# A two-layer mixer and MLP network: modulation sections 3 and 4 computed during attention, branch products spaced by gates, the context's last two MLP groups summed in PSUM

## The chip, the cores and the metric

The kernel runs on one core of a Trainium2 chip. The metric is the device time of one execution in microseconds (us), the median of several runs. The engines are named as in the profile: PE (TensorE, matrix products), DVE (VectorE), ACT (ScalarE), POOL (GpSimd) and SP (SyncE, which issues the DMAs, in order, from one queue).

## What is computed

512 latent tokens and 256 context tokens, 1024 wide, pass through two layers. Each layer has a mixing part with three branches (pooling, windowed attention whose latent queries also read the context, and a convolution module), merged by sigmoid gates, and a dense MLP. Both are modulated by six vectors that a product of the conditioning vector with `w_mod` gives.

```python
for i in range(DEPTH):                              # 2 layers
    mod_l = silu_c @ w_mod[i] + b_mod[i]            # six sections of 1024; mod_c likewise
    hl = _modulate(xl, sh1_l, sc1_l)                # layer norm, scale, shift
    ul_pool, ul_q, ul_k, ul_v, ul_conv, ul_gate = _split_in(hl @ w_in[i] + b_in[i])
    ...
    # _merge: (g_pool * y_pool + g_attn * y_attn + g_conv * y_conv) @ w_out
    xl = _post_norm(xl, g1_l, yl, ln1_g[i], ln1_b[i])
    yl = _mlp(_modulate(xl, sh2_l, sc2_l), w_mlp1[i], b_mlp1[i], w_mlp2[i], b_mlp2[i])
    xl = _post_norm(xl, g2_l, yl, ln2_g[i], ln2_b[i])
    # the context stream does the same in layer 0 only
```

## The kernel before

**Products.** Activations lie transposed in two parts, high and low (`actah`, `actal` and `actbh`, `actbl`), each weight tile likewise (`wh` by ACT, L134; `wl` by DVE or POOL, L137, as `ring["on"]` says). Each product is three matmuls: high by high, low by high, high by low. L156 is the matmul of `mm_a_steps`, whose output has features on the partitions: 512 latent tokens in one 512-column matmul, the context in a 256-column one. L165 to L167 are `mm_b_steps`, with tokens on the partitions. Raw weights come in tiles of 256 KB (`raw`, L129).

**Order on PE.** The order is made while the program is written out. Work comes as generators that yield the matmul columns they have issued; `tick` counts them. `later(cols, steps)` puts a generator in a list to be resumed once that many columns have passed. `pace(steps, every)` takes one step of a side generator every so many columns. `cover(cols)` issues steps of `other` (the gates and branch products) for so many columns.

**Modulation.** `mod_steps` (L173) multiplies one section of `w_mod` with the conditioning vector: eight chunks of k, and in each four matmuls of 32 by 256 (L185) into four strips of one PSUM bank; `chunk()` gives the tile for the weights. In layer 0, section 2 is paced through the first part of the mixing, and sections 3 and 4 through the tail stage (L824), in tiles of 512 KB; the six chunks left at its end follow in one run of 24 matmuls (L838).

**Mixing.** `w_phase` runs projections, rotary embedding and splits of q (L676, L677) and k (L710 to L714) on DVE and ACT, starts the convolution (53 scalar-tensor operations a stream on DVE, L323), and issues `other` until that is through. `pool_products` (L722) has its own small products. Then attention blocks run two at a time, their steps interleaved with `other`. The iterator `gated_steps` (L624) first makes eight gates for the attention branch and stores them (`sgd`), then alternates a gate of 24 matmuls a stream (`gate_steps`; bank of `psg`, evicted by ACT's tanh, L611) with a branch product of the pooling or the convolution branch (`branch_steps`; bank of `psa`, evicted by DVE, L621, the gate applied at once). In layer 1 two pooling gates are made ahead (`ahead`). POOL adds the two gated products (L641), and SP stores the sum (`mfd`, L642). Behind attention comes what I call the tail stage: `other` is drained, and eight attention branch products are made (L827 to L835).

**MLP.** `m_phase` runs `mlp1` (features on partitions, relu squared by ACT and DVE) and `mlp2` (tokens on partitions, summed group by group into `acc`, L970) for eight groups of four feature tiles (`GRP`). At the last group but one the sum is multiplied with the gate (L972, DVE) and the residual added (L973, POOL); at the last group follow L976, L977, statistics (L981) and `post`, the layer norm, and `norm_mod`, the modulation for the next layer, whose chain goes DVE (`rs`, L261), POOL (L262), DVE (L263), ACT (L278), PE transposes (L285). In layer 0 the latent tiles are finished first (`outer=True`), and the context's tiles 4 and 5 get groups 7 and 6 behind them (L1038, L1041).

## Time and profile before

| | us |
|---|---|
| runs, median (lowest, highest; 3 runs) | 1978.15 (1974.14, 1978.68) |
| profiled execution, its own time | 1975.67 |
| its span in the trace | 1973.9 |
| PE busy in it | 1848.6 (94%) |
| DVE, POOL, ACT busy | 1200.3, 771.6, 730.8 |
| stage: mixing of layer 0 up to the convolution's end, attention, tail stage | about 0 to 205, 205 to 478, 478 to 544 |
| stage: mixing of layer 1 | about 1212 to 1530 |

PE is busy for 94 percent of the span, and the chain that ended last runs through PE most of the time. A group of instructions is read as line, engine, operation, output from inputs, shape, count. In a wait the receiving instruction stands on the left of the arrow and what released it on the right. In a window, busy time stands engine by engine with its count, then the granted clock as a share of 2.4 GHz (0.50 is 1.2 GHz).

### The profile page before, as it was taken

How to read it: one execution, taken by the hardware profiler on the slowest of the kernel's cores; microseconds unless marked ns; L12 is line 12 of the kernel's file. 1: busy time of each engine (PE TensorE's matmuls, PEld its weight loads, DVE VectorE, ACT ScalarE, POOL GpSimd, SP SyncE). 2: the span in 40 equal slices, each digit the busy share in tenths (PEclk: the TensorE clock that was granted, in tenths of full speed). 3: DMA queues.
4: the chain of work that ended last, by engine and by line, in shares of the span. 5: the costliest groups of instructions: out<-in, count | busy, mean ns of one | idle time of the engine just before them, and what ended most of it. 6: DMA issues, size and time to landing. Idle time of an engine off the chain costs nothing. (4 is left out here: it accounts for less than half of the span.)

```text
span 1973.9 us, 27007 instructions
## 1 busy us (share of the span) xinstructions
PE 1848.6 (94%) x9910; PEld 1548.4 (78%) x9910; DVE 1200.3 (61%) x2067; ACT 730.8 (37%) x1359; POOL 771.6 (39%) x629
## 2 busy tenths in 40 slices
PE   6999899899899999999999988999988989999997
PEld 4788788787678888888788868777866768888886
DVE  6489655654478946865533584786575784333356
ACT  4432255353234422233133344434444354333331
POOL 3653432322434422222122546664342554333343
PEclk8999999999999999999999989999999989999999
DMA  8523111114865434464422423141212753332341
GB/s 304 176 90 118 62 59 46 53 44 154 281 219 190 161 112 133 155 213 143 146 62 86 129 96 105 61 149 63 69 65 96 260 189 118 96 96 86 107 129 43
DMA packets 117557, 244.94 MB, mean 124 GB/s; under 512 B 14608, under 2 KB 16944, under 8 KB 117424
## 3 DMA queue, kind: packets, MB, share of 16 engines
q1 hardware_dynamic: 117424, 243.21, 38.0%
q8 instruction: 78, 1.28, 0.3%
q14 instruction: 55, 0.45, 0.1%
HBM read 223.20 MB, written 19.96 MB: 123 GB/s over the span
## 5 line engine op out<-in xcount | busy, mean ns | idle before, releaser
L137 POOL TENSOR_TENSOR wl<-raw,wh 128x512 fp32r<-128x512 f32 x371 | 516.7, 1405 | 783.6 <-ACT wh L134 698.9
L134 ACT CAST wh<-raw 128x512 fp32r<-128x512 f32 x506 | 310.8, 621 | 596.0 <-PE ps L167 292.1
L156 PE MATMUL ps<-actbh,wh 128*128 128x512 f32 (+1 forms) x1016 | 353.4, 348 | 14.3 <-DVE sg L621 6.9
L156 PE MATMUL ps<-actbl,wh 128*128 128x512 f32 (+1 forms) x1016 | 348.3, 343 | 3.1 <-POOL actbl L251 3.1
L156 PE MATMUL ps<-actbh,wl 128*128 128x512 f32 (+1 forms) x1016 | 347.8, 342 | 2.7 <-DVE rs L261 1.3
L156 PE MATMUL ps<-actah,wh 128*128 128x512 f32 (+1 forms) x928 | 331.4, 357 | 13.7 <-ACT actah L248 4.7
L156 PE MATMUL ps<-actal,wh 128*128 128x512 f32 (+1 forms) x928 | 327.4, 353 | 3.3 <-DVE actal L1097 1.9
L156 PE MATMUL ps<-actah,wl 128*128 128x512 f32 (+1 forms) x928 | 326.9, 352 | 0.4 <-POOL wl L137 0.3
L156 PEld LDWEIGHTS ps<-actbh,wh 128*128 128x128 f32 x1016 | 194.5, 191 | 45.2 <-DVE sg L621 10.0
L156 PEld LDWEIGHTS ps<-actbh,wl 128*128 128x128 f32 x1016 | 194.4, 191 | 25.6 <-DVE wl L137 2.4
L156 PEld LDWEIGHTS ps<-actbl,wh 128*128 128x128 f32 x1016 | 194.6, 192 | 23.3 <-POOL actbl L251 3.8
L156 PEld LDWEIGHTS ps<-actah,wh 128*128 128x128 f32 x928 | 177.5, 191 | 43.8 <-ACT actah L248 5.1
L156 PEld LDWEIGHTS ps<-actal,wh 128*128 128x128 f32 x928 | 177.6, 191 | 25.6 <-DVE actal L1097 2.2
L156 PEld LDWEIGHTS ps<-actah,wl 128*128 128x128 f32 x928 | 177.4, 191 | 24.2 <-POOL wl L137 1.0
L165 PE MATMUL ps<-wh,actah 128*128 128x512 f32 x480 | 192.6, 401 | 2.2 <-DVE acc L977 2.0
L167 PE MATMUL ps<-wh,actal 128*128 128x512 f32 x480 | 190.5, 397 | 3.5 <-DVE actal L251 3.5
L166 PE MATMUL ps<-wl,actah 128*128 128x512 f32 x480 | 190.1, 396 | 0.0
L137 DVE TENSOR_TENSOR wl<-raw,wh 128x512 fp32r<-128x512 f32 x135 | 127.8, 947 | 99.9 <-ACT wh L134 97.3
L204 DVE SCALAR_TENSOR_TENSOR wm<-wm,sc,wm 128x512 f32<-128x512 f32 x140 | 124.4, 924 | 67.1 <-DMA wm<-in_wmod 67.0
L970 DVE TENSOR_TENSOR acc<-ps,acc 128x512 f32<-128x512 f32 x140 | 94.7, 684 | 95.3 <-PE ps L167 95.2
L165 PE MATMUL ps<-wh,actbh 128*128 128x512 f32 (+1 forms) x328 | 127.2, 388 | 1.5 <-DVE fg L621 1.5
L166 PE MATMUL ps<-wl,actbh 128*128 128x512 f32 (+1 forms) x328 | 126.8, 387 | 1.0 <-POOL wl L137 1.0
(207 smaller groups left out, 2721.7 us busy)
## 6 DMA issues: line engine op xcount, KB each, us to landing
raw<-in_w SPq DMA_DIRECT2D x264, 256.0 KB
raw<-in_win SPq DMA_DIRECT2D x154, 256.0 KB
wm<-in_wmod SPq DMA_DIRECT2D x72, 512.0 KB
raw<-in_wout SPq DMA_DIRECT2D x56, 256.0 KB
wm<-in_wmod SPq DMA_DIRECT2D x48, 256.0 KB
raw<-in_wbr SPq DMA_DIRECT2D x32, 256.0 KB
x1d<-R SPq DMA_DIRECT2D x10, 512.0 KB
acc<-in_b SPq DMA_DIRECT2D x10, 512.0 KB
```

What stands on the lines that cost most here:

```text
L134: S.copy(wh, r)
L137: e.tensor_tensor(out=wl, in0=r, in1=wh[:].bitcast(F32), op=ALU.subtract)
L156: T.matmul(ps, w(hl, w0 + n), x[xi][:, k, sl], start=(start and first and hl == 0 and xi == 0), stop=(stop and last and hl == 1))
L165: T.matmul(ps, x[0][:, k0 + k, tsl], wh, start=(k == 0), stop=False)
L166: T.matmul(ps, x[0][:, k0 + k, tsl], wl, start=False, stop=False)
L167: T.matmul(ps, x[1][:, k0 + k, tsl], wh, start=False, stop=(k == n - 1))
L204: V.scalar_tensor_tensor(out=o, in0=x, scalar=sc[:, k, r:r + 1], in1=o, op0=ALU.mult, op1=ALU.add)
L970: V.tensor_add(a, ps, a)
```

## The change

Six edits belong together.

- Sections 3 and 4 of layer 0 leave the tail stage. They are paced at 3500 columns through the attention of layer 0, in weight tiles of 256 columns (128 KB, three buffers), and `mod_steps` yields behind every matmul when tiles are that small, so each of the 64 stands by itself.
- A branch product is cut into pieces (one stream each), put in the list `pend`, and issued one piece behind each gate portion, into a bank of `psg`. The two gates that layer 1 made ahead are gone.
- The high copies of q and k move from DVE to ACT, and the low part of k is subtracted once and copied by ACT the second time.
- `context_end` runs groups 7 and 6 of tiles 4 and 5 into four PSUM banks without a sum in between; `finish` is what stood at the end of `mlp2`.
- In layer 1 a fifth tile of `w1` is computed on each half of the tokens at the beginning of the MLP (`NEXTRA` 8 instead of 6).
- The attention's `t1` shares a buffer, and `ot` has one instead of two.

```diff
@@ -43,7 +43,7 @@
 W_PT = 5000
 W_CN = 10000
 W_PV = 1800
-NEXTRA = (4, 6)
+NEXTRA = (4, 8)
 W_CHAIN = ((51000, 33000, 45000, 45000, 45000, 45000),
            (30000, 42000, 30000, 30000),
@@ -66,6 +66,7 @@
 ON_C = "G"
 MODVC = ()
 W_VAL = 9000
+EV_MOD = 3500
 W_CONV0 = 145000
 W_CONV1 = 118000
 T_POOL, T_Q, T_K, T_V, T_A, T_B, T_G = 0, 2, 6, 7, 8, 10, 12
@@ -158,13 +159,13 @@
                              stop=(stop and last and hl == 1))
                 yield 3 * (sl.stop - sl.start)
-    def mm_b_steps(ps, x, k0, n, tsl, w, cs=slice(0, 512)):
+    def mm_b_steps(ps, x, k0, n, tsl, w, cs=slice(0, 512), start=True, stop=True):
         for k in range(n):
             wh, wl = w[k][0][:, cs], w[k][1][:, cs]
-            T.matmul(ps, x[0][:, k0 + k, tsl], wh, start=(k == 0), stop=False)
+            T.matmul(ps, x[0][:, k0 + k, tsl], wh, start=(start and k == 0), stop=False)
             T.matmul(ps, x[0][:, k0 + k, tsl], wl, start=False, stop=False)
-            T.matmul(ps, x[1][:, k0 + k, tsl], wh, start=False, stop=(k == n - 1))
+            T.matmul(ps, x[1][:, k0 + k, tsl], wh, start=False, stop=(stop and k == n - 1))
             yield 3 * (cs.stop - cs.start)
     modT = {}
@@ -184,6 +185,8 @@
                 o = (j * q) % w.shape[-1]
                 T.matmul(ps[32 * j:32 * j + 32, :q], sc[:, k, :], w[:, o:o + q],
                          start=(k == 0), stop=(k == KD - 1))
+                if w.shape[-1] == q and j < 3:
+                    yield
             yield
         mod_finish(i, s, c0, n, ps, row)
         yield
...
@@ -591,7 +595,7 @@
             psg = ph.enter_context(tc.tile_pool(name=f"psg{i}", bufs=2, space=PSUM, reuse_waits="tile"))
             pss = mix.enter_context(tc.tile_pool(name=f"pss{i}", bufs=2, space=PSUM, reuse_waits="tile"))
             if todo:
-                pace((x for s in todo for x in mod_steps(i, s, 0, D, lambda: mg.tile(
+                pace((x for s in todo[:1] for x in mod_steps(i, s, 0, D, lambda: mg.tile(
                     [P, W], F32, tag="sg", name=uid("wm"))[:, :512])), 10000, 20000)
             def proj(t, sls):
@@ -600,7 +604,10 @@
                 drain(mm_a_steps(w, A, range(KD), o))
                 return [x[0] for x in o]
-            def gate_steps(m, b):
+            pend = []
+
+            def gate_steps(m, b, w2=None, ks=(), done=None):
+
                 t = KD * b + m
                 w = weight_a(I["win"][i, T_G + t])
@@ -609,12 +616,22 @@
                     ps = bank(psg)[:, :sl.stop - sl.start]
                     yield from mm_a_steps(w, A, range(KD), [(ps, sl)])
                     S.activation(g[:, sl], ps, AF.Tanh, bias=bg[:, t:t + 1], scale=0.5)
+                    if pend:
+                        yield from pend.pop(0)
+                if w2:
+                    pend.extend(piece(w2, ks, ks[0], g, o, done if o is outs_all[-1] else None)
+                                for o in outs_all)
                 return g
-            def branch_steps(w, ks, w0, g, outs, pool):
-
+            def piece(w, ks, w0, g, o, done):
                 while ks[0] not in mixed:
                     yield None
+                yield from branch_steps(w, ks, w0, g, [o], psg)
+                if done:
+                    done(g)
+
+            def branch_steps(w, ks, w0, g, outs, pool):
+
                 for _, sl in outs:
                     ps = bank(pool)[:, :sl.stop - sl.start]
                     yield from mm_a_steps(w, B, ks, [(ps, sl)], w0)
@@ -626,22 +643,26 @@
                     g = yield from gate_steps(m, 1)
                     nc.sync.dma_start(out=sgd[m], in_=g)
-                w, d, e, ahead = {}, {}, {}, 0 if todo else 2
-                for m in range(ahead):
-                    d[m] = yield from gate_steps(m, 0)
+                w, d = {}, {}
+
+                def merge(m, e):
+                    G.tensor_tensor(out=d[m], in0=d[m], in1=e, op=ALU.add)
+                    nc.sync.dma_start(out=mfd[m], in_=d.pop(m))
+
                 for m in range(KD + 1):
-                    if m + ahead < KD:
-                        d[m + ahead] = yield from gate_steps(m + ahead, 0)
                     if m < KD:
-                        w[m] = weight_a(I["wbr"][i, m][:, 0:4 * P])
-                        yield from branch_steps(w[m], (0, 1), 0, d[m], outs_all, side["bank"])
+                        w[m] = weight_half(m)
+                        d[m] = yield from gate_steps(m, 0, w[m], (0, 1))
                     if m:
-                        e = yield from gate_steps(m - 1, 2)
-                        yield from branch_steps(w.pop(m - 1), (2, 3), 2, e, outs_all, side["bank"])
-                        G.tensor_tensor(out=d[m - 1], in0=d[m - 1], in1=e, op=ALU.add)
-                        nc.sync.dma_start(out=mfd[m - 1], in_=d.pop(m - 1))
-
-            mixed, side = set(), {"bank": psa}
+                        yield from gate_steps(m - 1, 2, w.pop(m - 1), (2, 3), lambda e, m=m: merge(m - 1, e))
+                while pend:
+                    yield from pend.pop(0)
+
+            def weight_half(m):
+                w = weight_unit(I["wbr"][i, m][:, 0:4 * P])
+                return lambda hl, k: w[hl][:, k * P:(k + 1) * P]
+
+            mixed = set()
             other = gated_steps()
             def cover(cols):
@@ -673,7 +694,7 @@
                     r = slice(64 * par, 64 * par + 64)
                     ro = slice(64 - 64 * par, 128 - 64 * par)
                     q = Q[2 * jj + par]
-                    V.tensor_copy(q[r, :W], qf[r, :W])
+                    S.copy(q[r, :W], qf[r, :W])
                     V.tensor_tensor(out=q[ro, :W], in0=qf[r, :W], in1=q[r, :W].bitcast(F32),
                                     op=ALU.subtract)
@@ -707,11 +728,11 @@
             rope(scratch("rt")[:, :TL], kf, cs)
             for g in range(NKV):
                 r = slice(64 * g, 64 * g + 64)
-                V.tensor_copy(KH[g][r, :], kf[r, :])
-                S.copy(KH[g][64 - 64 * g:128 - 64 * g, :], kf[r, :])
-                for r2 in (0, 64):
-                    V.tensor_tensor(out=KL[g][r2:r2 + 64, :], in0=kf[r, :],
-                                    in1=KH[g][r, :].bitcast(F32), op=ALU.subtract)
+                r2 = slice(64 - 64 * g, 128 - 64 * g)
+                S.copy(KH[g][r, :], kf[r, :])
+                S.copy(KH[g][r2, :], kf[r, :])
+                V.tensor_tensor(out=KL[g][r, :], in0=kf[r, :], in1=KH[g][r, :].bitcast(F32), op=ALU.subtract)
+                S.copy(KL[g][r2, :], KL[g][r, :].bitcast(F32))
             Q = [kv.tile([P, W], F32R, tag=f"q{a}", name=uid("q")) for a in range(4)]
             query(Q, 0, 0, scratch("rt")[:, :TL])
             pu = proj(T_POOL + 1, LC)
@@ -752,6 +773,12 @@
             mixed.add(2)
             t12.close()
             pp = mix.enter_context(tc.tile_pool(name=f"pp{i}", bufs=1, side="right", reuse_waits="tile"))
+
+            if todo:
+                for _ in pe["pace"]:
+                    pass
+                pace((x for s in todo[1:] for x in mod_steps(i, s, 0, D, lambda: pp.tile(
+                    [P, 256], F32, tag="wm", name=uid("wm"), bufs=3))), EV_MOD)
             def items():
                 for g in range(NKV):
@@ -819,10 +846,6 @@
             ring["on"] = "GV"
             fin = ph.enter_context(tc.tile_pool(name=f"fin{i}", bufs=3, reuse_waits="tile"))
-            side["bank"] = psg
-            if todo:
-                pace((x for s in (3, 4) for x in mod_steps(i, s, 0, D, lambda: fin.tile(
-                    [P, D], F32, tag="wm", name=uid("wm"), bufs=4))), 9000)
             drain(other)
             for m in range(KD):
                 w = weight_a(I["wbr"][i, m][:, 4 * P:8 * P])
...
@@ -975,22 +998,50 @@
                 for cs, ps in zip(parts, pss):
                     V.tensor_mul(ps, ps, gb[tt // 4][:, hs_][:, cs])
                     V.tensor_add(a[:, cs], ps, a[:, cs])
-                st = sts[tt]
...
+                finish(tt, h)
+
+        def finish(tt, h):
+
+            hs_ = slice(h * 512, (h + 1) * 512)
+            a, st = acc[tt][:, hs_], sts[tt]
+            m = st.shape[1] // 2
+            for n in range(m):
+                V.bn_stats(st[:, h * m + n, :], a[:, n * 512 // m:(n + 1) * 512 // m])
+            if done[tt, 1 - h] < NGRP:
+                return
+            post(acc[tt], sts[tt], lng, lnb, POST if not last else TAIL3 if tt == NT - 1 else TAIL)
...
+
+        def context_end(g, ws):
+
+            tts = range(4, NT)
+            pss = {(tt, h): bank(psb) for tt in tts for h in range(2)}
+            for gg, first in ((g, True), (g - 1, False)):
+                for h in range(2):
+                    if (gg, h) not in ws:
+                        ring["early"] = E_B
+                        ws[gg, h] = [weight_unit(I["w2"][i, gg, h, k]) for k in range(GRP)]
+                        ring["early"] = 0
+                    for tt in tts:
+                        ps, hs_ = pss[tt, h], slice(h * 512, (h + 1) * 512)
+                        drain(mm_b_steps(ps, A, (gg * GRP) % (2 * GRP), GRP, slice(tt * P, (tt + 1) * P),
+                                         ws[gg, h], start=first, stop=not first))
+                        done[tt, h] += 1
+                        if not first:
+                            x1 = half(x1d[tt], h)
+                            V.tensor_add(ps, ps, acc[tt][:, hs_])
+                            V.tensor_mul(ps, ps, gb[1][:, hs_])
+                            V.tensor_add(acc[tt][:, hs_], ps, x1)
+                            finish(tt, h)
+                    del ws[gg, h]
         done = {}
@@ -1001,13 +1052,18 @@
         w2s = {}
         for n, sl in enumerate([slice(0, 256), slice(256, 512)] + ([CS] if has_ctx else [])):
             ready(2 if n == 0 or (n == 1 and has_ctx) else 0)
-            for f in range(len(w)):
+            for f in range(GRP):
                 mlp1(f, [sl], w[f])
-            if n == 0 and not has_ctx:
-                mlp2(0, w2s, range(2), (0,))
+            if not has_ctx:
+                if n == 0:
+                    mlp2(0, w2s, range(2), (0,))
+                    w.append(weight_a(I["w1"][i, GRP]))
+                mlp1(GRP, [sl], w[GRP])
             if n == 1 and has_ctx:
                 w.append(weight_a(I["w1"][i, GRP]))
                 mlp1(GRP, [LS], w[GRP])
+            if n == 2:
+                mlp1(GRP, [sl], w[GRP])
         ring["on"] = "GGV"
         if todo:
             pace((x for a in todo for x in mod_sums_steps(*a, lambda: bcp.tile(
@@ -1035,11 +1091,7 @@
                 mlp2(g, w2s, range(4), outer=True)
                 if has_ctx:
                     ring["on"] = ON_C
-                    mlp2(g, w2s, range(4, NT))
-                    w2s = {}
-                    ring["early"] = E_B
-                    mlp2(g - 1, w2s, range(4, NT))
-                    ring["early"] = 0
+                    context_end(g, {k: v for k, v in w2s.items() if k[0] == g})
             w2s = {k: v for k, v in w2s.items() if k[0] >= g}
             for f in range(1, GRP):
                 if g + 1 < NGRP:
@@ -1138,7 +1190,7 @@
         pre = {"ps": pres, "close": psp.close}
         for i in range(DEPTH):
             last = i == DEPTH - 1
-            w_phase(i, A, B, not last, pre, () if i else (2,))
+            w_phase(i, A, B, not last, pre, () if i else (2, 3, 4))
             todo = [] if last else [(i, 5)] + [(i + 1, s) for s in range(6)]
             pre = m_phase(i, A, B, not last, last, todo)
             A, B = B, A
```

**Order of PE.** In the tail stage of the kernel before, around one k-chunk of a section (`wm` are its weights, `ps_5192` a branch product's or gate's bank):

```order
L156 MATMUL ps_5192<-actbl,wh_5184 128x512
L156 MATMUL ps_5192<-actbh,wl_5185 128x512
L185 MATMUL ps_4886<-wm_5202,sc 32x256 x4
L156 MATMUL ps_5192<-actbh,wh_5184 128x512
L156 MATMUL ps_5192<-actbl,wh_5184 128x512
L156 MATMUL ps_5192<-actbh,wl_5185 128x512
L156 MATMUL ps_5212<-actbh,wh_5184 128x256
```

In the attention of layer 0 of the kernel after, around the first matmul of section 3 (`pt` are transposes of attention weights, L157 is the former L156, L186 the former L185):

```order
L435 MATMUL pt_2850<-ident_66,P_2564 128x128
L435 MATMUL pt_2850<-ident_66,P_2593 128x128
L435 MATMUL pt_2850<-ident_66,P_2641 128x128
L435 MATMUL pt_2850<-ident_66,P_2663 128x128
L186 MATMUL ps_2566<-wm_2867,sc 32x256
L157 MATMUL ps_2824<-actah,wh_2813 128x512
L157 MATMUL ps_2824<-actal,wh_2813 128x512
L157 MATMUL ps_2824<-actah,wl_2814 128x512
L157 MATMUL ps_2824<-actah,wh_2819 128x512
```

The four matmuls of a chunk stood together between 128-wide products; now one stands alone between transposes and a gate's products, and the next follows ten rows on.

**Order of DVE.** At the end of layer 0's MLP in the kernel before, from the last of tile 3's statistics on (`acc_6294` and `acc_6295` are the context's tiles 4 and 5, `rs_10898` is tile 3's):

```order
L972 TENSOR_TENSOR acc_6294<-acc_6294,g_1794_10192 128x512
L259 BN_AGGR mv_10896<-st_10893 128x2
L972 TENSOR_TENSOR acc_6295<-acc_6295,g_1794_10192 128x512
L261 TENSOR_SCALAR rs_10898<-mv_10896 128x1
L970 TENSOR_TENSOR acc_6294<-ps_10964,acc_6294 128x512
L263 SCALAR_TENSOR_TENSOR rs_10898<-mv_10896,rs_10898 128x1
L970 TENSOR_TENSOR acc_6295<-ps_10982,acc_6295 128x512
L972 TENSOR_TENSOR acc_6294<-acc_6294,g_1794_10192 128x512
L972 TENSOR_TENSOR acc_6295<-acc_6295,g_1794_10192 128x512
```

The same place in the kernel after (`ps_11000`, `ps_11002` are PSUM sums of both groups, `acc_6390` is tile 4):

```order
L262 BN_AGGR mv_10992<-st_10989 128x2
L264 TENSOR_SCALAR rs_10994<-mv_10992 128x1
L266 SCALAR_TENSOR_TENSOR rs_10994<-mv_10992,rs_10994 128x1
L1040 TENSOR_TENSOR ps_11000<-ps_11000,acc_6390 128x512
L1041 TENSOR_TENSOR ps_11000<-ps_11000,g_1842_10288 128x512
L1042 TENSOR_TENSOR acc_6390<-ps_11000,xh_11136 128x512
L1009 BN_STATS st_10298<-acc_6390 128x6
L1040 TENSOR_TENSOR ps_11002<-ps_11002,acc_6391 128x512
L1041 TENSOR_TENSOR ps_11002<-ps_11002,g_1842_10288 128x512
```

The context's L970 and L972, which stood among tile 3's statistics, are gone, and `rs` of tile 3 follows its `mv` without anything between; the context's three operations for each bank come behind it.

## Rows read from the trace of the kernel before

**Rows 1.** Stages: PE, PEld, DVE, ACT, POOL busy (count); clock; DMA share; GB/s.

```profile
120.00:200.00 80.00, 80.00 (x460) 69.93 (x459) 77.56 (x141) 20.88 (x37) 37.86 (x32) 1.00 0.29 92
205.00:478.00 273.00, 252.92 (x1497) 218.27 (x1496) 156.35 (x331) 121.12 (x262) 86.44 (x76) 0.99 0.17 55
478.60:544.20 65.60, 58.07 (x389) 42.75 (x390) 26.99 (x38) 17.04 (x26) 29.35 (x18) 0.96 0.86 297
1680.00:1880.00 200.00, 200.00 (x884) 165.60 (x884) 70.30 (x99) 66.58 (x109) 62.45 (x48) 1.00 0.32 95
```

**Rows 2.** Timeline of PE (start, duration in us): four 32x256 matmuls at 101.

```profile
101.03 0.39 PE L156 MATMUL ps<-actah,wl 128*128 128x512 f32 x1
101.35 0.64 PE L185 MATMUL ps<-wm,sc 128*32 128x256 f32 x8
...
102.26 0.39 PE L156 MATMUL ps<-actal,wh 128*128 128x512 f32 x1
```

**Rows 3.** Timeline of PE around eight 32x256 matmuls at 722.

```profile
722.44 0.39 PE L156 MATMUL ps<-actbh,wl 128*128 128x512 f32 x1
...
724.10 0.40 PE L156 MATMUL ps<-actbl,wh 128*128 128x512 f32 x1
```

**Rows 4.** Waits of PE, tail stage: us in total, times, longest.

```profile
PE ps L185 <- DMA wm<-in_wmod: 7.4, 4, 3.1
```

**Rows 5.** Groups of PE, tail stage: count, busy us, mean ns, idle before.

```profile
L156 PE MATMUL ps<-actbh,wh 128*128 128x512 f32 x34 | 14.5, 426 | 0.1
...
L156 PE MATMUL ps<-actbh,wh 128*128 128x256 f32 x35 | 10.1, 289 | 1.3 <-DVE fg L621 1.3
```

**Rows 6.** DMA of the tail stage: total; issues with KB each.

```profile
DMA packets 7179, 19.49 MB, mean 297 GB/s; under 512 B 900, under 2 KB 1028, under 8 KB 7172
...
wm<-in_wmod SPq DMA_DIRECT2D x13, 512.0 KB
```

**Rows 7.** Waits of PE, attention of layer 0.

```profile
PE ps L156 <- DVE sg L621: 6.9, 8, 2.5
PE S L501 <- ACT P L515: 3.4, 1, 3.4
PE ps L156 <- ACT qf L665: 2.6, 3, 1.0
PE ps L734 <- DVE pwh L250: 2.4, 1, 2.4
```

**Rows 8.** Window in that attention: PE busy (count), clock, DMA share, GB/s.

```profile
376.00:379.00 3.00, 3.00 (x10) 0.50 0.00 0
```

**Rows 9.** Groups of DVE, 120 to 212 us.

```profile
L676 DVE CAST q<-qf 64x768 fp32r<-64x768 f32 x4 | 3.6, 906 | 0.1
```

**Rows 10.** Waits of PE, end of layer 0's MLP.

```profile
PE ps L285 <- ACT acc L278: 7.2, 2, 4.7
```

**Rows 11.** Timeline of DVE, end of layer 0's MLP.

```profile
1176.70 1.67 DVE L972 TENSOR_TENSOR acc<-acc,g 128x512 f32<-128x512 f32 x1
...
1178.35 0.67 DVE L970 TENSOR_TENSOR acc<-ps,acc 128x512 f32<-128x512 f32 x1
1181.25 1.21 DVE L263 SCALAR_TENSOR_TENSOR rs<-mv,rs 128x1 f32<-128x1 f32 x1 [2.23 <-POOL rs L262]
```

**Rows 12.** Timeline of POOL, same place.

```profile
1177.77 1.72 POOL L973 TENSOR_TENSOR acc<-acc,xh 128x512 f32<-128x512 f32 x1
1179.45 1.26 POOL L137 TENSOR_TENSOR wl<-raw,wh 128x512 fp32r<-128x512 f32 x1
```

**Rows 13.** Waits of PE, mixing of layer 1.

```profile
PE S L501 <- DVE q L677: 5.5, 1, 5.5
...
PE ps L736 <- POOL pwl L251: 2.1, 1, 2.1
...
PE ps L156 <- DVE sg L621: 2.0, 1, 2.0
```

**Rows 14.** Waits of SP's queue, 215 to 560 us.

```profile
SPq L642 <- POOL sg L641: 33.8, 8, 7.8
```

More of the change, by code (lines that the diff above doesn't have):

```diff
@@ L453, in softmax_pv @@
             yield 1024 * len(ns), W_PV
[L454 removed]
+        t1 = pp.tile([P, 512], F32R, tag="pth", name=uid("pth"), bufs=2)[0:64, :].bitcast(F32)
+        t1 = t1.rearrange("p (a q) -> p a q", a=4)
         S.copy(t1, po[64:128, :].rearrange("p (a q) -> p a q", a=4))
[L456 removed]
+        ot = pp.tile([P, 2, P], F32, tag="ot", name=uid("ot"), bufs=1)
         top = po[0:64, :].rearrange("p (a q) -> p a q", a=4)
@@ L836, in w_phase @@
             if todo:
-                for _ in pe["pace"]:
+                for _ in pe["pace"] or ():
                     pass
```

26 lines of the change are left out of this document (9 added, 17 removed).

## Prediction

> **What bounds the kernel now.** I read the busy time by stage first [rows 1]. Between 1680 and 1880 us TensorE (PE) is busy for all of 200 us with 884 matmuls, most of 512 columns, so a 512-column matmul costs 0.226 us at the full clock (2.4 GHz), and the only way to shorten such a stretch is to give PE less. PE is the bound elsewhere too, but with holes: 273.0 us of layer 0's attention hold 252.9 busy, and 65.6 us of the stage behind it (below: the tail stage) hold 58.1 at a DMA share of 0.86. So the change is a question of PE's holes: those that it closes, those that it opens, and the PE work that it adds. I then went through the waits of PE stage by stage, with the timelines where PE changes from one kind of matmul to another.
>
> **Sections 3 and 4, the price on PE.** The weights of one k-chunk of a section meet the conditioning vector in four matmuls of 32 by 256. Before, they stand four together. At 101 us [rows 2] the last 512-column matmul ahead of the four starts at 101.03 and the second one behind them at 102.26; without them these would lie two steps apart, 0.45, so the four cost 0.78. Two sets of four in a row at 722 us [rows 3] cost 1.66 less 0.45, 1.21: the second set adds 0.43. So 0.35 of the 0.78 is the change between the two kinds of matmul and 0.43 is streaming, in which the four run side by side. The change puts each matmul alone between 128-wide ones (order of PE, above). A single isn't in this trace. Its bounds are 0.43 (streaming, the change of kind free) and 0.78 (as much as four). I take 0.757, near the upper end, because four side by side already cost what one must stream. 64 singles: 64 x 0.757 = **+48.4 us** (27.5 to 49.9). Before, ten sets of four and one run of six sets cost 10 x 0.78 + 0.78 + 5 x 0.43 = 10.7; they go with the stage below.
>
> The Trainium skill says in "TensorEngine Tiling (Array Packing)", Key Properties, that a change of the tiling mode drains the engine, and that tiles in different places of the array run in parallel. By it a lone tile pays the drains of four and shares its stream with nobody, which speaks against this part of the change: the 64 would cost their upper bound, 49.9, and the sum below would be -1.8 in place of -3.3. The trace agrees with the rule in the 0.35 and in the 0.43 for four at once; of a single no run here shows it yet.
>
> **The tail stage without them.** Its PE work without sections is 126 matmuls of 512 columns (34 x 3 in one form [rows 5] and 8 x 3 in another) and 129 of half that (35 x 3 and 8 x 3): 126 x 0.226 + 129 x 0.113 + 0.9 for the rest = 44.0. It takes 65.6. Of the difference PE's waits for a section's weights are 7.4 in four places [rows 4], the first of which ends where the window begins; it is at most the longest, 3.1, and I add half of that: 65.6 - 44.0 + 1.5 = **-23.1**. What is late next: the stage moved 19.49 MB [rows 6], of which 13 section loads of 512 KB are 6.8; the rest, with the first layer's output weights, is some 13 MB, 43 us at 297 GB/s, level with PE's 44.0. I take **+2** for what stays uncovered (0 to 8: at 250 GB/s it is 52).
>
> **Where the singles go in.** They are spaced 3500 columns apart behind the convolution, in some 130 us of attention. What PE waits for there [rows 7] it can spend on singles, if one stands just ahead of the wait. The scores wait 3.4 for the masked product of ACT, the query projections 2.6 for ACT's eviction; behind the 3.4 wait the granted clock was 0.50, the level of 1.2 GHz, from 376 to 379 us [rows 8], so 3 us held the work of 1.5, and with the rest of that stretch about 2 are lost there. With small waits of 0.4 behind them I take **-8.5** as absorbed by about eleven singles (0 to -12). The other 53 singles find PE busy.
>
> **Branch products spaced.** Each gate (24 matmuls a stream) is followed by one piece of six of a branch product that waits only for a bank of its own pool of two. Before, a branch product follows its predecessor into the attention's bank: eight waits for DVE's evictions (`sg`, L621), 6.9 in all [rows 7], and about 2 of low clock behind the longest (2.5). With a gate between, they go: **-9** (-6 to -10). In their place gate and piece share two banks: a piece of 256 columns takes 6 x 0.113 = 0.7, and the gate behind it needs the bank that ACT must empty within that time. No row shows it; there are sixteen such places, a wait of the old kind was 6.9 / 8 = 0.9, and I take a sixth of that for each: **+2.5** (0 to 6).
>
> **q and K splits to ACT.** DVE is busy 77.6 of 80 us before 200 [rows 1]. Four copies of 0.906 [rows 9], two copies and two subtractions of K that are no narrower leave it for ACT, which is busy 20.9 of those 80: 8 x 0.906 = 7.2, and DVE is done that much earlier. PE's wait for `pwh` (2.4 [rows 7]) goes with about 2 of low clock: **-4.5** (-2 to -5). ACT's idle time hides the same work there; without it the 7.2 would come back.
>
> **The end of the context's MLP.** At tile 3 PE waits 4.7 for the normalised rows (7.2 with the wait for tile 2 [rows 10]). Followed back: ACT waits for DVE's `rs` at 1181.25, which waited 2.23 for POOL [rows 11], and POOL was at L973 (1.72, context) and a weight's low part (1.26 [rows 12]). DVE had an L972 of 1.67 in the way as well. With the two groups summed in PSUM the four L970, L972 and L973 ahead of the last sums are gone; `rs` follows its statistics directly (order of DVE, above). The 4.7 and some 2.4 of low clock, as behind the 3.4 wait above, go; what is late next is the bank: four are held at once, and three DVE operations of 0.67, the time of L970 at 1178.35, free each where two did: +0.7. **-6.4** (-3 to -8).
>
> **Layer 1's mixing.** The early DVE copies matter again: the second query's 5.5 wait for `q` [rows 13] shortens by the two copies on its path (2 x 0.6, the 0.906 taken by width, 512 of 768) and as much again of low clock, a little rounded up, -3; the 2.1 for `pwl` goes, -2.2; the 2.0 for `sg` goes with the spacing, -2. The gates no longer run two ahead, so ten gates are issued before the first branch product is allowed, and the tail of attention has one fewer uncovered group, -1.9; the new two-bank sharing and the copies on ACT give back 2. **-7** (-2 to -10).
>
> **MLP of layer 1, and the rest.** The fifth tile splits 24 matmuls of 512 columns into 48 of half: **+0.3** (0 to 1). It stands behind the work for which PE waits at the start, so that wait stays. The shared buffers (`t1`, `ot`) cost nothing: the attention product that fills them next comes some us later.
>
> **Loads of the singles.** They are 64 DMAs of 128 KB from SP's one queue, three buffers deep. SP waits there for POOL's gated sums (`mfd` stores, 33.8 in eight, longest 7.8 [rows 14]), and behind such a wait a section load stands too. Three buffers are three spacings, 3 x (1.6 + 0.76) = 7.1 us ahead, so only the longest bites: **+2** (0 to 16).
>
> **The sum**: 48.4 - 23.1 + 2 - 8.5 - 9 + 2.5 - 4.5 - 6.4 - 7 + 0.3 + 2 = -3.3. The profiled execution took 1975.7, so 1972.4; the median of the runs is 2.5 above it and would give 1974.9. I forecast **1973**, between the two, with 1966 to 1981 as this case's own range.
>
> **Rivals.** (1) *Cheap singles.* The change of kind overlaps the matmuls beside it, and a single costs its stream alone: 64 x 0.43 = 27.5 in place of 48.4, so 1952. For it: the four start side by side, and PE loads weights beside matmuls. Against it: 0.35 is left over in every set of four. (2) *Slower: singles in full.* PE is the bound throughout attention and singles stand between the waits, not ahead of them: the 8.5 isn't absorbed, and the 4.5 of `pwh` reappears as the next PE wait; 1986. It decides if fewer than four of the 64 singles stand directly ahead of a PE wait of over 0.7. For it: 252.9 of 273.0 busy. Against it: the 3.4 and the 2.6 of [rows 7] come in the very stretch where the singles begin. (3) *Slower: loads late.* Sixteen of 64 section loads come 1 us late behind `mfd` stores and raw weights: 1973 + 16, 1989. For it: 33.8 us of SP waits; against it: DMA share 0.17. (4) *The tail stage doesn't become PE-bound*: the DMA runs at 240 GB/s in it, +8, 1981; the change then doesn't do there what it says.
>
> **How the numbers follow.** A measurement of this kernel can tell 0.3%, 5.9 us, so 1972.2 and 1984.1 bound "the same". The forecast has 0.49, about 0.21 of it below 1972.2 and 0.28 above; rival 1 0.21 (faster), rival 2 0.17 and rival 3 0.08 (slower), rival 4 0.05 (same). Faster 0.42, same 0.33, slower 0.25. The range leaves out the far half of rivals 1 and 3: 1952 to 1988.
>
> **What would show it.** Singles: the second matmul behind one stands 1.2 behind the one ahead (0.88 in rival 1). Tail stage: 45 to 48 us long. No wait of over 1 for `sg` in layer 0's attention; none for `pwh`; the tile-3 wait at the context's end under 1. Wrong if PE waits for `wm` by over 5 in attention, if the tail stage is longer than 52, or if the singles cost under 0.5.

## The result, and the profile after

The changed kernel takes 2001.17 us (1999.98 to 2002.32), the kernel before 1976.14 in the same comparison: a ratio of 1.0129, 95% interval 1.0107 to 1.0152. The forecast was 1973, and its range ended at 1988. The profiled execution has a span of 1998.1 us, 24.2 more than before.

A change of many parts is first cut at places that both traces have. I used four PE matmuls: the first one of the pooling products (`pwh`) in each layer, and the first one of the output projection (`wout`) in each. Columns are the time from the mark before, in us, for the kernels whose profiles are compared here; the last one ends at the start of PE's last matmul.

| | to pooling product, layer 0 | to `wout`, layer 0 | MLP of layer 0, to pooling product, layer 1 | to `wout`, layer 1 | to PE's last matmul |
|---|---|---|---|---|---|
| before | 204.6 | 338.7 | 781.4 | 225.6 | 412.9 |
| after | 210.3 | 351.5 | 791.9 | 217.9 | 415.8 |
| difference | +5.7 | +12.8 | +10.5 | -7.7 | +2.9 |

The second and fourth column came out about as the prediction's terms had it. The losses that nobody had forecast stand in the first column and the third, ahead of the pooling products of each layer. The third column also holds the context's end, which was to shorten it. Cut once more, at the last `mlp2` matmuls of layer 0, its MLP is 1.2 us shorter, and the part from there to layer 1's pooling product 11.7 longer (131.3 to 143.0). The edit that the first column and this last part share is the move of q's and K's copies to ACT.

What PE waits for in layer 0 in the kernel after (in total, times, longest; the rows that answer to [rows 7]), and the longest waits in layer 1 from 1300 us (to [rows 13]):

```profile
PE ps L157 <- ACT sg L618: 7.2, 4, 6.1
PE ps L354 <- DVE cn L348: 2.3, 3, 1.5
PE ps L157 <- ACT qf L686: 2.0, 3, 1.0
PE ps L186 <- DMA wm<-in_wmod: 1.8, 1, 1.8
...
PE ps L157 <- DVE sg L638: 0.9, 2, 0.5
PE ps L755 <- DVE pwh L253: 0.9, 1, 0.9
```

```profile
PE ps L157 <- ACT sg L618: 8.0, 1, 8.0
PE ps L455 <- DVE ptl L449: 3.5, 6, 1.8
PE ps L354 <- DVE cn L348: 3.0, 1, 3.0
PE ps L755 <- DVE pwh L253: 2.0, 1, 2.0
PE S L505 <- DVE q L698: 1.5, 2, 1.2
```

DVE's `sg` (6.9 before) is 0.9, the 3.4 for `P` is gone, and the loads of the singles (`wm`) make PE wait once, at the start. In place of all that stand two waits that were not there: 6.1 and 8.0 us for `sg` of ACT, the tanh by which ACT empties a gate's bank (PE waited 0.5 for it in layer 0 before). PE's timeline (start, duration) shows the first, and a window behind it the granted clock (the column behind POOL's busy time):

```profile
142.59 0.28 PE L157 MATMUL ps<-actah,wl 128*128 128x256 f32 x1
148.99 0.80 PE L157 MATMUL ps<-actah,wh 128*128 128x512 f32 x1 [6.13 <-ACT sg L618]
149.59 0.63 PE L157 MATMUL ps<-actal,wh 128*128 128x512 f32 x1
```

```profile
146.60:153.40 6.80, 4.41 (x10) 3.51 (x11) 6.71 (x12) 3.69 (x6) 2.52 (x2) 0.50 0.36 102
```

The granted clock was 0.50 (1.2 GHz) from 146.6, while PE still waited, to 153.4. So PE, having waited, ran its first 4.4 us at half its clock, which cost some 2.2 more. Now ACT over the same time and, behind the dots, in layer 1; then DVE in layer 0, for which ACT waits:

```profile
134.97 0.47 ACT L686 ACTIVATE qf<-ps,b_in 128x256 f32<-128x256 f32 x1
146.55 1.68 ACT L697 CAST q<-qf 64x768 fp32r<-64x768 f32 x2 [11.11 <-DVE qf L412]
148.25 0.69 ACT L618 ACTIVATE sg<-ps,bg 128x512 f32<-128x512 f32 x1
...
1305.80 1.26 ACT L697 CAST q<-qf 64x512 fp32r<-64x512 f32 x2 [13.69 <-DVE qf L412]
1307.08 0.69 ACT L618 ACTIVATE sg<-ps,bg 128x512 f32<-128x512 f32 x1
```

```profile
139.15 0.76 DVE L326 SCALAR_TENSOR_TENSOR cp<-gl,cvec,cp 128x512 f32<-128x512 f32 x1
...
142.82 0.75 DVE L411 TENSOR_TENSOR qf<-qf,cs 128x512 f32<-128x512 f32 x1
143.49 0.74 DVE L326 SCALAR_TENSOR_TENSOR cp<-gl,cvec,cp 128x512 f32<-128x512 f32 x1
144.72 1.73 DVE L412 TENSOR_TENSOR qf<-qf,rt 128x512 f32<-128x512 f32 x1 [0.49 <-POOL rt L410]
```

ACT evicts q at 134.97 and then stands for 11.11 us, though it has the gate's tanh to do: PE is done with the gate's 512-wide matmuls at 140.0 and with its 256-wide ones, in the second bank, at 142.9, and then finds no bank free. Next in ACT's queue is the copy of q (L697), and that needs the rotary embedding, which DVE does between operations of the convolution until 146.4. The tanh starts at 148.25, directly behind the copy, and PE goes on 0.7 later. Layer 1 shows the same, with 13.69. In the kernel before the copy stood on DVE itself, behind the embedding in the same queue, and didn't hold ACT's.

The other large parts. A single section matmul, in the attention of layer 0 of the kernel after:

```profile
380.07 0.40 PE L455 MATMUL ps<-ptl,V 128*128 128x512 f32 x1
380.40 0.62 PE L186 MATMUL ps<-wm,sc 128*32 128x256 f32 x2
380.95 0.50 PE L157 MATMUL ps<-actah,wh 128*128 128x512 f32 x1
381.29 0.40 PE L157 MATMUL ps<-actal,wh 128*128 128x512 f32 x1
```

From 380.07 to 381.29 are 1.22 us; two plain steps would be 0.45, so one matmul costs 0.77, as much as four did [rows 2]. And the tail stage, from the last matmul of attention to `wout` (before: 69.1 us):

```profile
514.50:561.80 47.30, 46.99 (x271) 41.18 (x270) 22.70 (x36) 14.20 (x21) 27.65 (x16) 1.00 0.79 263
```

It is 47.8 us long, PE busy in all but 0.3 of the 47.3 of this window, the DMA at 263 GB/s.

### The profile page after: what moved, and what is told of

It reads as the page before. It is cut to its first block, busy times and chain, and to the rows that moved or that the text cites. A ratio compares the mean times of both kernels' runs of the same rounds, so it can differ in the third digit from the quotient of the medians.

```text
span 1998.1 us, 27117 instructions
## 1 busy us (share of the span) xinstructions
PE 1881.0 (94%) x9934; PEld 1555.7 (78%) x9934; DVE 1170.8 (59%) x2040; ACT 750.0 (38%) x1385; POOL 763.4 (38%) x626
## 5 line engine op out<-in xcount | busy, mean ns | idle before, releaser
L157 PE MATMUL ps<-actbh,wh 128*128 128x512 f32 (+1 forms) x1016 | 352.3, 347 | 11.5 <-ACT sg L618 8.3
L157 PE MATMUL ps<-actah,wh 128*128 128x512 f32 (+1 forms) x936 | 339.2, 362 | 19.0 <-ACT sg L618 7.0
L157 PE MATMUL ps<-actbl,wh 128*128 128x512 f32 (+1 forms) x1016 | 348.2, 343 | 4.4 <-POOL actbl L254 4.4
L157 PE MATMUL ps<-actbh,wl 128*128 128x512 f32 (+1 forms) x1016 | 347.6, 342 | 1.9 <-POOL wl L138 1.2
L157 PE MATMUL ps<-actal,wh 128*128 128x512 f32 (+1 forms) x936 | 329.4, 352 | 3.8 <-DVE actal L1149 2.1
L157 PE MATMUL ps<-actah,wl 128*128 128x512 f32 (+1 forms) x936 | 328.9, 351 | 0.4 <-POOL wl L138 0.3
L157 PEld LDWEIGHTS ps<-actah,wh 128*128 128x128 f32 x936 | 179.1, 191 | 68.8 <-issue 25.6
L157 PEld LDWEIGHTS ps<-actbh,wh 128*128 128x128 f32 x1016 | 194.9, 192 | 39.8 <-ACT sg L618 9.2
L157 PEld LDWEIGHTS ps<-actbl,wh 128*128 128x128 f32 x1016 | 195.0, 192 | 25.0 <-POOL actbl L254 5.1
L157 PEld LDWEIGHTS ps<-actbh,wl 128*128 128x128 f32 x1016 | 194.7, 192 | 24.5 <-POOL wl L138 1.6
L157 PEld LDWEIGHTS ps<-actal,wh 128*128 128x128 f32 x936 | 179.4, 192 | 25.8 <-POOL actal L254 3.0
L157 PEld LDWEIGHTS ps<-actah,wl 128*128 128x128 f32 x936 | 179.2, 191 | 24.3 <-POOL wl L138 1.0
L138 DVE TENSOR_TENSOR wl<-raw,wh 128x512 fp32r<-128x512 f32 x134 | 123.8, 924 | 95.8 <-ACT wh L135 95.4
L207 DVE SCALAR_TENSOR_TENSOR wm<-wm,sc,wm 128x512 f32<-128x512 f32 x140 | 128.4, 953 | 66.3 <-DMA wm<-in_wmod 65.8
```

The lines of the kernel that those rows point to most:

```text
L138: e.tensor_tensor(out=wl, in0=r, in1=wh[:].bitcast(F32), op=ALU.subtract)
L157: T.matmul(ps, w(hl, w0 + n), x[xi][:, k, sl], start=(start and first and hl == 0 and xi == 0), stop=(stop and last and hl == 1))
L207: V.scalar_tensor_tensor(out=o, in0=x, scalar=sc[:, k, r:r + 1], in1=o, op0=ALU.mult, op1=ALU.add)
```

## The experiments

**The suspected cause, alone and undone.** Four runs, compared with the same runs of the kernel before (1975.6 us; runs 5 to 8 have 1977.8 beside them, runs 9 to 11 have 1977.4).

Run 1 puts q's copies back:

```diff
-                    S.copy(q[r, :W], qf[r, :W])
+                    V.tensor_copy(q[r, :W], qf[r, :W])
```

> The kernel after, with the 16 high copies of q put back from ACT to DVE; the copies of K stay on ACT. Theory A (ACT's in-order queue is held by a q copy that waits for DVE's rotary embedding behind the convolution, so the gates' evictions come late): PE's waits for sg by ACT's tanh fall from 7.2 us in layer 0 and 8.0 us in layer 1 to under 1 each, the low clock behind them (about 2.2 and 3.0) goes too, and some 2 to 4 us of the wait for pwh come back: 2001 - 20 + 3 = 1984 us (1981 to 1988). Rival R1 (ACT simply has too much work there, with K's copies as much as q's): half of it, about 1992. Rival R2 (the waits come from the two banks that gates share): no change, 2001.

Measured: 1985.43 us (ratio to the kernel before 1.0056, 1.0037 to 1.0076), 15.7 less than the kernel after. The two long waits are gone: between 120 and 580 us, and from 1290 to 1420, the first lines are now

```profile
PE ps L354 <- DVE cn L348: 2.3, 3, 1.5
PE ps L157 <- ACT qf L686: 2.0, 3, 1.0
PE ps L186 <- DMA wm<-in_wmod: 1.8, 1, 1.8
PE ps L157 <- DVE sg L638: 1.1, 2, 0.7
PE ps L157 <- ACT sg L618: 1.1, 3, 0.6
```

```profile
PE ps L354 <- DVE cn L348: 3.0, 1, 3.0
PE ps L755 <- DVE pwh L253: 2.0, 1, 2.0
PE ps L455 <- DVE ptl L449: 1.1, 2, 0.9
```

The first pooling product starts at 205.0 instead of 210.3, and from the last `mlp2` matmuls of layer 0 to layer 1's pooling product it takes 134.7 instead of 143.0. Together these are 13.5 us. That the sharing of banks makes the wait (R2) is out. Two other differences of the profiles nearly cancel: 4.6 less in layer 0's MLP, where the two kernels are alike, and 5.7 more in layer 1's attention (223.6 instead of 217.9), where PE waits longer for the late q copies, now on DVE too (1.5 in the kernel after):

```profile
PE S L505 <- DVE q L698: 4.5, 2, 3.6
```

Run 2 puts K's splits back as well:

```diff
-                S.copy(KH[g][r, :], kf[r, :])
+                V.tensor_copy(KH[g][r, :], kf[r, :])
                 S.copy(KH[g][r2, :], kf[r, :])
-                V.tensor_tensor(out=KL[g][r, :], in0=kf[r, :], in1=KH[g][r, :].bitcast(F32), op=ALU.subtract)
-                S.copy(KL[g][r2, :], KL[g][r, :].bitcast(F32))
+                for r3 in (0, 64):
+                    V.tensor_tensor(out=KL[g][r3:r3 + 64, :], in0=kf[r, :],
+                                    in1=KH[g][r, :].bitcast(F32), op=ALU.subtract)
```

> The kernel after, with the splits of q and K both as in the kernel before (DVE). Theory A: K's copies were not what held ACT, so within 4 us of the run with q alone put back: 1984 us (1980 to 1988), pwh wait about 2.5 as before. Rival R1 (ACT's amount of work): another 8 us below the run with q alone. Rival R2: 2001.

Measured: 1993.26 us (1.0093, 1.0071 to 1.0114). A miss of all theories: 8 slower than run 1, not the same and not faster. That ACT simply has too much work (R1) is out, since without K's copies it got no faster. The waits that the prediction had hoped to close are back (pooling products, 2.6 in layer 0; 2.1 beside the 2.0 in layer 1):

```profile
PE ps L756 <- DVE pwh L253: 2.6, 1, 2.6
...
PE ps L758 <- POOL pwl L254: 2.1, 1, 2.1
PE ps L756 <- DVE pwh L253: 2.0, 1, 2.0
```

Of the 7.8 us, 5.3 lie in layer 1 between its first pooling product and `wout` (table below), where the 2.1 stands; 3.2 lie in layer 0's MLP, where the two kernels are alike, and are not this edit's. The 5.3 are hardly waiting: PE is idle there for 20.0 us in place of 19.3, but its mean granted clock is 0.94 in place of 0.97. And layer 0 up to `wout` is 1.3 shorter than in run 1, in spite of the 2.6. So K's copies on ACT cost nothing that shows, and the loss is q's; that K's gain anything, as the prediction described, isn't settled.

Run 3 is the kernel before with the two hunks on q and K alone.

> The kernel before, with only the splits of q and K moved to ACT as the change does. Theory A: PE waits for sg by ACT's tanh of about 6 and 8 us appear in the two layers, with low clock behind them: 1976 + 17 = 1993 us (1989 to 1997). What the prediction took (-4.5 in layer 0 and some 5 in layer 1): 1967. Rival R2 (the wait needs the new sharing of banks by gates and pieces): 1967 to 1976.

Measured: 1989.77 us (1.0069, 1.0040 to 1.0097), 13.6 slower than the kernel before; expected 17, with 1989 to 1997. The waits for ACT's tanh are there without any other part of the change:

```profile
...
PE ps L156 <- ACT sg L611: 6.6, 2, 6.1
```

```profile
PE ps L156 <- ACT sg L611: 8.0, 1, 8.0
```

```profile
148.21 1.68 ACT L676 CAST q<-qf 64x768 fp32r<-64x768 f32 x2 [11.10 <-DVE qf L409]
149.92 0.69 ACT L611 ACTIVATE sg<-ps,bg 128x512 f32<-128x512 f32 x1
```

This settles it: the 6.1 and the 8.0, and an ACT queue held for 11.1, come with this edit alone. The stages show where (table below): 7.6 more up to layer 0's pooling product, 8.4 more in the third column (12.9 more ahead of layer 1's pooling product, 4.5 less in the MLP, where the two kernels are alike), but 3.8 less in layer 0's attention, where the wait of 3.4 for `P` is gone.

**What a section matmul costs.** Run 4 issues two instead of one at a time:

```diff
-EV_MOD = 3500
+EV_MOD = 7000
...
-                if w.shape[-1] == q and j < 3:
+                if w.shape[-1] == q and j == 1:
                     yield
```

> The kernel after, with the section matmuls in attention two at a time (a step behind every second one, spaced 7000 columns in place of 3500; tiles and buffers as they are). By the price that the trace of after shows for a single (second matmul behind it 1.22 us after the one ahead, 0.77 over plain spacing) and shows before for four together (0.78): 32 x 0.78 in place of 64 x 0.77, 24 us less, 1977 us (1973 to 1982). Rival (a single is cheap and its cost is its stream, 0.43): 2001 - 64 x 0.43 + 32 x 0.43 = 1987. Rival (absorbed anyway): 2001.

Measured: 1977.32 us (1.0009, 0.9995 to 1.0022), 23.9 less than the kernel after, where 24.6 was expected and 13.8 by the rival. A pair in its trace:

```profile
282.65 0.40 PE L455 MATMUL ps<-ptl,V 128*128 128x512 f32 x1
282.98 0.63 PE L186 MATMUL ps<-wm,sc 128*32 128x256 f32 x4
283.53 0.50 PE L157 MATMUL ps<-actah,wh 128*128 128x512 f32 x1
283.87 0.39 PE L157 MATMUL ps<-actal,wh 128*128 128x512 f32 x1
```

282.65 to 283.87 is 1.22 us again: two cost what one does. Thirty-two changes of kind less at 0.77 are the whole gain. That doesn't yet say that waits absorbed nothing: 32 pairs may close as much waiting as 64 singles (run 8).

**Only the early q copies.** If the copy hurts because DVE is busy with the convolution, the second four q tiles, made in attention, may stay on ACT:

```diff
-                    S.copy(q[r, :W], qf[r, :W])
+                    (S.copy if g else V.tensor_copy)(q[r, :W], qf[r, :W])
```

> The kernel after, with the high copies of the first four q tiles (made while DVE still runs the convolution) put back on DVE; those of the second four, made during attention, and K's stay on ACT. Theory A says that only a copy that waits for a busy DVE holds ACT, so the early part should be as short as with all q copies back (205 us to the first pooling product, against 210 in the kernel after), and layer 1's attention as short as in the kernel after (218 us from the first pooling product to the output projection, against 224 with all q copies back): 1985 - 6 = 1979 us (1975 to 1984). Rival (ACT is held in attention as well): 1985 or above.

Measured: 1979.64 us (1.0011, 0.9996 to 1.0027), 205.4 us to the first pooling product and 221.8 for layer 1's attention, where 218 was expected. So the time came out as expected in part by luck: of the 8.7 us between the profiles of runs 1 and 5, 1.8 lie in layer 1's attention and 5.9 in the third column, where the two kernels are alike. Run 6 adds run 4's pairs:

> The same with the section matmuls in pairs. Both effects are in different stages and should add: 1979 - 24 = 1955 us (1950 to 1961), faster than the kernel before by 0.8 to 1.3%. Rival (they share a wait): above 1965.

Measured: 1954.78 us (0.9885, 0.9867 to 0.9904). The two effects add (24.9 between runs 5 and 6), and the rest of the change is then faster than the kernel before.

**Other terms, one at a time.** Run 7 is the kernel before with `finish`, `context_end` and their call:

> The kernel before, with only the context's last two groups summed in PSUM. The prediction's term: -6.4 (-3 to -8), so 1969 us, the wait of 4.7 for tile 3's normalised rows gone. Rival (the time is given back at the start of layer 1, where DVE and POOL wait for the same chain): 1974 to 1977.

Measured: 1970.85 us (0.9970, 0.9957 to 0.9983): -5.9 us, -8.5 to -3.4. PE's waits for normalised rows there, 7.2 before with 4.7 for tile 3's, are

```profile
PE ps L285 <- ACT acc L278: 3.7, 2, 2.5
```

so that 1.2 is left of the 4.7. Run 8 is the kernel after with the sections in the tail stage:

```diff
-                pace((x for s in todo[1:] for x in mod_steps(i, s, 0, D, lambda: pp.tile(
-                    [P, 256], F32, tag="wm", name=uid("wm"), bufs=3))), EV_MOD)
...
+                pace((x for s in (3, 4) for x in mod_steps(i, s, 0, D, lambda: fin.tile(
+                    [P, D], F32, tag="wm", name=uid("wm"), bufs=4))), 9000)
```

> The kernel after, with sections 3 and 4 put back into the tail stage in tiles of 512 KB and sets of four, all else as in after. By the prediction's terms the move itself costs 48.4 - 23.1 + 2 - 8.5 + 2 = +20.8, so 2001 - 21 = 1980 us (1976 to 1985), and the tail stage takes 60 to 66 us again. Rival (the spacing of the branch products saves nothing in layer 0): 1987 to 1990 us.

Measured: 1979.44 us (1.0005, 0.9990 to 1.0021). The move into attention costs 2001.2 - 1979.4 = 21.7, and 21.3 in the one stage where the two kernels differ (351.5 against 330.2); the two ratios, which come from different comparisons, would make it 24.5. The tail stage is 71.1 us long. The attention ahead of it, from the pooling product to its last matmul, is 259.1 long, against 303.7 with the singles: 44.6 more, where 64 x 0.77 and a wait of 1.8 for `wm` would make 51. In it PE's waits other than for `wm` are 10.8 us in run 8, 7.4 with singles and 7.8 with pairs. So of the 6.5 that are missing some 3 go with shorter waits, with 32 pairs nearly as much as with 64 singles; where the rest went is open.

Run 9 is the kernel before with the spacing (`pend`, `piece`, `merge`) alone:

> The kernel before, with only the branch products spaced by gates (and without the two gates ahead in layer 1). The prediction's terms: -9 + 2.5 in layer 0, and -2 - 1.9 + 1 in layer 1, so 1977 - 9 = 1968 us (1964 to 1972). From the run of after with the sections in the tail stage (330.2 us from the first pooling product to layer 0's output projection, against 334.9 for the kernel before with q and K on ACT) the part of layer 0 is about -5. Rival (the spacing saves nothing: what it closes opens as waits for the two shared banks): 1975 to 1979.

Measured: 1975.77 us (0.9999, 0.9985 to 1.0012). A miss: no gain at all by itself. What PE waits for in layer 0's mixing in it:

```profile
...
PE ps L156 <- DVE sg L634: 5.4, 3, 4.1
PE ps L156 <- ACT qf L682: 2.6, 3, 1.0
PE ps L351 <- DVE cn L345: 2.3, 3, 1.5
PE ps L751 <- DVE pwh L250: 2.1, 1, 2.1
```

Eight waits for `sg` are three, but one of them is 4.1, at 373.5 us, where the scores' wait of 3.4 for `P` stood (now absent). DVE shows why:

```profile
366.85 2.62 DVE L693 CAST q<-qf 64x768 fp32r<-64x768 f32 x2
369.49 2.87 DVE L694 TENSOR_TENSOR q<-qf,q 64x768 fp32r<-64x768 f32 x2
372.37 0.16 DVE L512 SCALAR_TENSOR_TENSOR ngm<-mx,nsink 128x1 f32<-128x1 f32 x1
372.45 0.68 DVE L511 TENSOR_REDUCE mx<-S 128x1 f32<-128x512 f32 x1
373.05 0.41 DVE L634 SCALAR_TENSOR_TENSOR sg<-sg,ps 128x256 f32<-128x256 f32 x1
```

The second group's q copies and subtractions, 5.5 us of them, stand ahead of the eviction (L634). In the kernel after, where the copies are ACT's, the waits for this `sg` are 0.9 in all. But the copies' place alone doesn't decide it: in run 1, with the copies on DVE and singles in attention, they are 1.1. So without singles the eviction met the copies; with singles it didn't. The stage gains 3.0 (338.7 to 335.7), layer 1's mixing loses 2.1 (225.6 to 227.7), though PE is idle there for less (19.0 us in place of 23.3): its mean granted clock is 0.94 in place of 0.98.

**Sets of four, and the fifth tile.** Run 10 takes run 6 and issues four at a time. Two weight tiles of twice the width share the rotary embedding's buffers in attention:

```diff
...
-                    [P, 256], F32, tag="wm", name=uid("wm"), bufs=3))), EV_MOD)
+                    [P, TL], F32, tag="rt", name=uid("wm"), bufs=2))), EV_MOD)
...
```

> The run with late q copies on ACT and pairs, but the section matmuls four at a time, spaced 14000 columns, their weights in two tiles of 512 columns that share the rotary embedding's buffer. By the price of a set of four in the kernel before (0.78) 16 x 0.78 in place of 32 x 0.78: 12.5 less than 1955, 1942 us (1938 to 1949). Rival (sharing the buffer makes the rotary embedding wait, or a set of four is late with its two loads): 1950 to 1960, with waits of PE for wm or q.

Measured: 1951.37 us (0.9861, 0.9840 to 0.9883), runs between 1944.9 and 1953.0: a miss, outside the 1938 to 1949 expected and in the rival's range, though the waits that the rival named hardly grew (2.4 for `wm`, 1.5 for `q` in layer 1, where the kernel after has 1.8 and 1.5). The stage where the sections are gained 8.9 of the expected 12.5 (327.9 to 319.0); the profile took 6.2 more than run 6's between `wout` and the end of the context's MLP, where nothing was changed. Run 11 is run 10 without the fifth tile:

> The same as the run with sets of four, without the fifth tile of w1 at the start of layer 1's MLP. The prediction's term for that tile: +0.3 (0 to 1), so 1942 as well, within 2 us of the run with sets of four. Rival (the fifth tile does cover part of the waits of 4.8 and 3.1 at that start): 3 to 6 us slower than the run with sets of four.

Measured: 1943.91 us (0.9848, 0.9825 to 0.9870). The intervals of runs 10 and 11 overlap, and of the 9.4 us between their profiles 6.1 lie in the third column, where they are alike, so the tile's effect isn't told apart from zero. That leaving it out costs 3 to 6 us, as the rival had it, doesn't show. The stages of the profiles:

| | to pooling, layer 0 | to `wout` | MLP and to pooling, layer 1 | to `wout`, layer 1 | to PE's last matmul |
|---|---|---|---|---|---|
| run 1, q back on DVE | 205.0 | 351.4 | 779.1 | 223.6 | 415.4 |
| run 2, q and K back | 203.3 | 351.9 | 782.6 | 228.9 | 415.5 |
| run 3, before, q and K on ACT | 212.2 | 334.9 | 789.8 | 226.6 | 412.5 |
| run 4, pairs | 213.2 | 328.3 | 786.7 | 220.1 | 412.9 |
| run 5, late q on ACT | 205.4 | 351.5 | 773.2 | 221.8 | 413.9 |
| run 6, late q on ACT, pairs | 203.7 | 327.9 | 777.4 | 219.6 | 413.2 |
| run 7, before, context's end | 203.2 | 338.8 | 779.0 | 225.0 | 412.8 |
| run 8, sections in tail | 213.8 | 330.2 | 791.3 | 220.0 | 415.7 |
| run 9, before, spaced | 206.1 | 335.7 | 783.1 | 227.7 | 413.4 |
| run 10, sets of four | 203.2 | 319.0 | 782.7 | 219.8 | 415.6 |
| run 11, no fifth tile | 203.2 | 319.3 | 776.6 | 218.6 | 413.3 |

The first column splits cleanly: 210 to 214 with the early q copies on ACT, 203 to 206 without. So does the part of the third from the last `mlp2` matmuls of layer 0 on: 143 to 144 with them, 131 to 136 without. A stage in which two kernels are alike differs by up to about 6 us in the third column, and by up to 4 elsewhere, between profiles.

## Why the prediction was wrong

The forecast was -3.3, the result +25. **The step that failed** is "q and K splits to ACT" with its sentence "ACT's idle time hides the same work there". It counted ACT's free time (busy 20.9 of 80 us, [rows 1]) and not its order. The copy of q needs DVE's rotary embedding, on the engine whose lateness the same paragraph had just named, and ACT waits for it with the next tanh behind it. Run 3 measures the edit alone at +13.6 (7.9 to 19.2), against -4.5 in layer 0 and some 5 of the -7 in layer 1 that rested on it: some 23 of the 28 us by which the forecast missed. Of the reasoning about K the waits bear out a part: in run 1, with its copies on ACT, no long wait for ACT is left, and with them back on DVE the 2.6 and 2.1 for `pwh` and `pwl` return (run 2), but layer 0 gets no longer by that. In layer 1's attention the late q copies gain what the prediction said: PE's wait for `q` is 1.5 with them on ACT and spacing, 4.5 in run 1 with spacing alone. The stage takes 217.9 to 221.8 in the kernels that have both, 223.6 in run 1.

Point by point:

- **Singles.** 48.4 predicted; 64 x 0.77 = 49 in the trace, and run 4's 23.9 for half of them. The Trainium skill says in "TensorEngine Tiling (Array Packing)", Key Properties, that a change of the tiling mode drains the engine and that different tiles can run in parallel. This case agrees: one, two and four matmuls of a set all cost 0.77 to 0.78.
- **Where singles go in.** -8.5 predicted as absorbed. In the result the waits of [rows 7] are gone but for 2.0 for `qf` and 0.9 each for `sg` and `pwh`, but most had other remedies: in run 8, without singles, the 3.4 is gone and DVE's `sg` down to 1.3 as well. Run 8 leaves some 3 us of waits to the singles, and 6.5 in all by the lengths. Rival 2's condition is met: behind the first single, PE waits over 0.7 only twice in that attention (0.97 and 0.78).
- **Tail stage.** -23.1 + 2, and 45 to 48 us long: 47.8, with 21.3 saved of 69.1. The prediction's window was shorter, 65.6; by it the stage would be some 44. The whole move, singles included, was +20.8 by the terms and is +21.7 by run 8.
- **Spacing.** -9 + 2.5 in layer 0, -3 in layer 1; by itself 0 (run 9). Five of the eight waits did go, but one of 4.1 came where `P` had been waited for, behind q's copies on DVE, which the prediction left out, and in layer 1 the lower clock took what the shorter waits gave. The 2 us of low clock that it counted behind the wait of 2.5 were not there: from 222 to 230, around that wait's end at 222.9, the granted clock was 1.00. With q and K on ACT, runs 8 and 3 differ by 10.3, of which the context's end is some 5.9; so some 4 may be the spacing's there, which isn't told apart from the fifth tile.
- **Context's end.** -6.4 predicted, -5.9 measured alone (run 7), by the chain that the prediction followed: 1.2 is left of the 4.7. In the kernel after it is 0.6; two waits for ACT's `acc` are left, 3.1 in all, where there were 7.2 [rows 10]. Some of it comes back: at the start of layer 1 PE waits 4.2 for POOL's `actbl` in both, against 1.7 before and 3.3 in runs 3 and 9, which lack this edit.
- **Layer 1's mixing.** -7 predicted, -7.7 from its pooling product on. The wait for `q` fell from 5.5 to 1.5 and the 2.0 for `sg` is gone; the 2.1 for `pwl` became 0.8, beside a new 2.0 for `pwh`. The 11.7 lost ahead of that product had no term.
- **Fifth tile.** +0.3 predicted; not told apart from 0.
- **Loads of the singles.** +2 predicted, 1.8 measured.

Measured parts: 21.7 (move) + 13.6 (q and K) - 5.9 (context's end) + 0 (spacing) = 29.4, against 25.0 for the whole. The 4.4 between are no more than these measurements' noise, or the 4 that the spacing may gain once q is on ACT. The rivals at 1986 and 1989 had the right sign. Rival 2 was right in part, that most of the 8.5 isn't absorbed; its other part, a wait for `pwh` that reappears, and the late loads of rival 3 aren't there, and neither names the copies, which made the most of the miss.

Slower, then, is the sum of one edit that costs more than it brings (singles, +21.7) and one that was to pay for it and cost as well (q's copies). With early q copies on DVE and the sections in sets of two or four, the same change is 1.2 to 1.4% faster than the kernel before (runs 6 and 10).

## What to carry to other kernels

An engine with idle time isn't free for work if its queue is in order: before moving an operation to it, ask what the operation waits for and what stands behind it. Here K's copies did no harm on the idle engine, and the late q copies, made in attention, none either (run 5); the early q copies, which wait for an engine that is itself late, held up what stood behind them and were better off on that engine.

A small matmul of another shape between large ones has a price by the interruption, here 0.77 us for one, two or four. If such work must be spread, spread it in the largest sets that the buffers hold.

## What the runs showed that was not expected

A wait of 6.1 us costs more than itself: the granted clock fell to 0.50 within it, and PE ran its first 4.4 us behind it at that clock.

Two kernels with the same code over layer 0's MLP differ there by some 6 us in a profile, and runs of one kernel differ by 8 us in all (1944.9 to 1953.0 in run 10). The profiles show what the difference consists of: between `wout` and the end of the context's MLP (640 to 650 us) PE waits for 18 to 24 us and has the clock at 0.50 for 10 to 31 us. Less the waits and half of that time, all thirteen profiles take 611 to 615. What sets the waits and the clock there was not found.
